# Row-wise min-max normalisation: groups of eight rows, stored whole, with VectorE kept in the written order

## Chip, cores and metric

One core of one Trainium2 chip. The metric is the device time of one execution in microseconds; a profile's span (first to last instruction) is about 1.8 us shorter. All runs quoted were in the fast state. A ratio is the mean time of one kernel's fast runs over that of the other's in the same rounds, so it is not quite the ratio of the medians quoted beside it.

## The reference

```python
def reference(x):                      # x: 32 x 512 x 1024, float32
    x_min = x.min(axis=-1, keepdims=True)
    x_max = x.max(axis=-1, keepdims=True)
    return ((x - x_min) / (x_max - x_min + 1e-8)).astype(np.float32)
```

That is 16,384 rows of 1024: 67.11 MB read once from HBM (the chip's main memory), 67.11 MB written once.

## The kernel before

Each tile has 4 rows on each of 128 partitions. GpSimd (POOL) issues the load, which casts to bf16 on the way. VectorE (DVE) halves the rows twice with a maximum and a minimum, then reduces. POOL adds and multiplies the per-row statistics, ScalarE (ACT) normalises row by row, SyncE (SP) issues two stores a tile. The order of VectorE's instructions is the scheduler's. The last 512 rows go in four small tiles.

```python
ROWS_PER_PART = 4; TT_LEVELS = 2; TAIL_TILES = 4
IN_BUFS = 7; OUT_BUFS = 4; STORE_SPLIT = 2
# ... pools cut ...
    def process(xview, oview, t, r, pool, store_rows):
        xt = pool.tile([P, r, d], bf16, name=f"xt_r{r}")
        nc.gpsimd.dma_start(out=xt, in_=xview[t])
        # ... two levels of tensor_tensor max / min, then two tensor_reduce (cut) ...
        nc.gpsimd.tensor_tensor(out=rng, in0=mx, in1=neg_mn, op=OP.add)
        nc.vector.reciprocal(out=inv, in_=rng)
        nc.gpsimd.tensor_tensor(out=nbias, in0=neg_mn, in1=inv, op=OP.mult)
        ot = out_pool.tile([P, r, d], fp32, name=f"ot_r{r}")
        for rr in range(r):
            nc.scalar.activation(out=ot[:, rr, :], in_=xt[:, rr, :], func=ACT.Identity,
                                 bias=nbias[:, rr : rr + 1], scale=inv[:, rr : rr + 1])
            if (rr + 1) % store_rows == 0:
                lo = rr + 1 - store_rows
                nc.sync.dma_start(out=oview[t, :, lo * d : (rr + 1) * d],
                                  in_=ot[:, lo : rr + 1, :])
    # ... views cut ...
    for t in range(T_main):
        process(xv, ov, t, R, in_pool, STORE_SPLIT)
    for t in range(TAIL_TILES):
        process(xvt, ovt, t, 1, tail_pool, 1)
```

Of the kernel before, what the change touches and what calls it, by code (L numbers as in the profile page):

```python
# [1 line left out]

# [4 lines left out]

ROWS_PER_PART = 4
TT_LEVELS = 2  # L10
TAIL_TILES = 4
IN_BUFS = 7
OUT_BUFS = 4
STORE_SPLIT = 2


@with_exitstack
def kernel(
    ctx: ExitStack,
    tc: tile.TileContext,  # L20
    x: bass.AP,
    out: bass.AP,
):
    nc = tc.nc
    fp32 = mybir.dt.float32
    bf16 = mybir.dt.bfloat16
    AX = mybir.AxisListType.X
    OP = mybir.AluOpType
    ACT = mybir.ActivationFunctionType

    P = nc.NUM_PARTITIONS
    R = ROWS_PER_PART

    x_flat = x.flatten_outer_dims()
    out_flat = out.flatten_outer_dims()
    n, d = x_flat.shape

    in_pool = ctx.enter_context(tc.tile_pool(name="in_pool", bufs=IN_BUFS))
    out_pool = ctx.enter_context(tc.tile_pool(name="out_pool", bufs=OUT_BUFS))
    tmp_pool = ctx.enter_context(tc.tile_pool(name="tmp_pool", bufs=2))  # L40
    stat_pool = ctx.enter_context(tc.tile_pool(name="stat_pool", bufs=10))
    tail_pool = ctx.enter_context(tc.tile_pool(name="tail_pool", bufs=TAIL_TILES + 1))

    def process(xview, oview, t, r, pool, store_rows):
        xt = pool.tile([P, r, d], bf16, name=f"xt_r{r}")
        nc.gpsimd.dma_start(out=xt, in_=xview[t])  # L46

        width = d
        cur_max = xt
        cur_min = xt  # L50
        for lvl in range(TT_LEVELS):
            half = width // 2
            nxt_max = tmp_pool.tile([P, r, half], bf16, name=f"ttmax{lvl}_r{r}")
            nc.vector.tensor_tensor(  # L54
                out=nxt_max,
                in0=cur_max[:, :, 0:half],
                in1=cur_max[:, :, half:width],
                op=OP.max,
            )
            nxt_min = tmp_pool.tile([P, r, half], bf16, name=f"ttmin{lvl}_r{r}")  # L60
            nc.vector.tensor_tensor(  # L61
                out=nxt_min,
                in0=cur_min[:, :, 0:half],
                in1=cur_min[:, :, half:width],
                op=OP.min,
            )
            cur_max, cur_min = nxt_max, nxt_min
            width = half

        mx = stat_pool.tile([P, r], fp32, name=f"mx_r{r}")  # L70
        nc.vector.tensor_reduce(out=mx, in_=cur_max, axis=AX, op=OP.max)  # L71
        neg_mn = stat_pool.tile([P, r], fp32, name=f"negmn_r{r}")
        nc.vector.tensor_reduce(  # L73
            out=neg_mn, in_=cur_min, axis=AX, op=OP.min, negate=True
        )

        rng = stat_pool.tile([P, r], fp32, name=f"rng_r{r}")
        nc.gpsimd.tensor_tensor(out=rng, in0=mx, in1=neg_mn, op=OP.add)  # L78
        inv = stat_pool.tile([P, r], fp32, name=f"inv_r{r}")
        nc.vector.reciprocal(out=inv, in_=rng)  # L80
        nbias = stat_pool.tile([P, r], fp32, name=f"nbias_r{r}")
        nc.gpsimd.tensor_tensor(out=nbias, in0=neg_mn, in1=inv, op=OP.mult)  # L82

        ot = out_pool.tile([P, r, d], fp32, name=f"ot_r{r}")
        for rr in range(r):
            nc.scalar.activation(  # L86
                out=ot[:, rr, :],
                in_=xt[:, rr, :],
                func=ACT.Identity,
                bias=nbias[:, rr : rr + 1],  # L90
                scale=inv[:, rr : rr + 1],
            )
            if (rr + 1) % store_rows == 0:
                lo = rr + 1 - store_rows
                nc.sync.dma_start(
                    out=oview[t, :, lo * d : (rr + 1) * d],
                    in_=ot[:, lo : rr + 1, :],
                )

    n_tail_rows = TAIL_TILES * P  # L100
    n_main_rows = n - n_tail_rows
    assert n_main_rows % (P * R) == 0
    T_main = n_main_rows // (P * R)

    xv = x_flat[0:n_main_rows].rearrange("(t p r) d -> t p (r d)", p=P, r=R)
    ov = out_flat[0:n_main_rows].rearrange("(t p r) d -> t p (r d)", p=P, r=R)
    for t in range(T_main):
        process(xv, ov, t, R, in_pool, STORE_SPLIT)

    xvt = x_flat[n_main_rows:n].rearrange("(t p r) d -> t p (r d)", p=P, r=1)  # L110
    ovt = out_flat[n_main_rows:n].rearrange("(t p r) d -> t p (r d)", p=P, r=1)
    for t in range(TAIL_TILES):
        process(xvt, ovt, t, 1, tail_pool, 1)


# [1 line left out]
_INS = ['x']  # L117
_OUTS = [((32, 512, 1024), 'float32')]


# [23 lines left out]
```

## Time and profile before

| | value | how to read it |
|---|---|---|
| time | 327.14 us (327.11 to 327.32) | median of 4 runs |
| span | 325.3 us | of the profiled execution |
| busiest engine | VectorE, 58% | no engine is the bound |
| 16 DMA engines | full but for the start, 20 to 31 us and the end | the bound |

The lines themselves stand in the prediction below, with what is to be seen in each. A DMA packet here is one contiguous run that one of the 16 DMA engines moves: 16 KB read for a load (8 KB written as bf16), 8 KB for a store. Shares and DMA busy times slightly over 100% come from the records of packets, which overlap a little in time.

### The profile page before, as it was taken

The page shows a single profiled execution, that of the slowest core. Times are in us where ns is not written, and L with a number is a line of the kernel's source. Part 1 is how long each engine was busy: PE and PEld are TensorE (multiplying, and loading weights), DVE is VectorE, ACT ScalarE, POOL GpSimd, SP SyncE. Part 2 cuts the span into 40 slices and gives each one's busy share as a digit, 9 for nine tenths or more (in the row PEclk, how much of TensorE's full clock was granted, in tenths as well). Part 3 has the DMA queues.
Part 4 walks back from the last instruction along what each step waited for, and adds up shares of the span by engine and source line. Part 5 has one row for each costly group of instructions (what it writes and reads, how often), then busy time and mean ns, then how long its engine had stood idle before and what let it go on. Part 6 is the DMA issues. An engine that isn't in the chain of part 4 may idle for free.

```text
span 325.3 us, 774 instructions
## 1 busy us (share of the span) xinstructions
DVE 190.0 (58%) x245; ACT 148.9 (46%) x129; POOL 60.9 (19%) x109
## 2 busy tenths in 40 slices
DVE  0899788533588443445677685577536789970000
ACT  0108953546050505235554245553355543999800
POOL 3174411210101102021101212012221042320000
DMA  6988999999999999999999999999999999999996
GB/s 124 214 178 165 282 282 299 329 309 312 285 288 279 283 284 285 288 313 313 315 312 340 314 334 295 313 329 326 333 314 312 309 334 360 430 425 429 425 430 286
DMA packets 14549, 100.71 MB, mean 310 GB/s; under 512 B 1616, under 2 KB 1616, under 8 KB 2640
## 3 DMA queue, kind: packets, MB, share of 16 engines
q0 software_dynamic: 5040, 33.56, 50.0%
q1 hardware_dynamic: 9504, 67.11, 49.8%
q14 instruction: 5, 0.04, 0.0%
HBM read 67.11 MB, written 67.11 MB: 413 GB/s over the span
## 4 chain that ended last, share of the span: by engine, by line
DMA 73%; ACT 13%; DVE 4%; issue 2%; POOL 1%; another core or an unknown queue 1%; ACTq 1%; PEldq 0%
DMA out_dram<-ot_r 71%; ACT ot_r L86 13%; DMA xt_r<-in_x_dram 2%; DVE ttmax_r L54 1%; DVE ttmin_r L61 1%; POOL rng_r L78 1%; DVE negmn_r L73 1%; DVE mx_r L71 1%; ACTq L139 0%; POOL xt_r L46 0%; ACTq L86 0%; POOL nbias_r L82 0%; PEldq L139 0%
## 5 line engine op out<-in xcount | busy, mean ns | idle before, releaser
L86 ACT ACTIVATE ot_r<-xt_r,nbias_r,inv_r 128x1024 f32<-128x1024 bf16 x128 | 147.7, 1228 | 149.5 <-DMA out_dram<-ot_r 134.9
L54 DVE TENSOR_TENSOR ttmax_r<-xt_r 128x2048 bf16<-128x2048 bf16 (+1 forms) x35 | 39.4, 1126 | 36.7 <-DMA xt_r<-in_x_dram 36.6
L46 POOL DMA_DIRECT2D xt_r<-in_x_dram x35 | 19.8, 566 | 140.1 <-ACT ot_r L86 138.9
L80 DVE RECIPROCAL inv_r<-rng_r 128x4 f32<-128x4 f32 (+1 forms) x35 | 6.1, 175 | 64.7 <-POOL rng_r L78 63.9
L71 DVE TENSOR_REDUCE mx_r<-ttmax_r 128x4 f32<-128x1024 bf16 (+1 forms) x35 | 39.1, 1117 | 0.0
L73 DVE TENSOR_REDUCE negmn_r<-ttmin_r 128x4 f32<-128x1024 bf16 (+1 forms) x35 | 39.1, 1116 | 0.0
L61 DVE TENSOR_TENSOR ttmin_r<-xt_r 128x2048 bf16<-128x2048 bf16 (+1 forms) x35 | 39.0, 1113 | 0.0
L82 POOL TENSOR_TENSOR nbias_r<-negmn_r,inv_r 128x4 f32<-128x4 f32 (+1 forms) x35 | 23.2, 666 | 40.7 <-DVE inv_r L80 40.6
L78 POOL TENSOR_TENSOR rng_r<-mx_r,negmn_r 128x4 f32<-128x4 f32 (+1 forms) x35 | 18.2, 520 | 49.7 <-DVE negmn_r L73 49.4
L61 DVE TENSOR_TENSOR ttmin_r<-ttmin_r 128x1024 bf16<-128x1024 bf16 (+1 forms) x35 | 22.3, 636 | 0.0
L54 DVE TENSOR_TENSOR ttmax_r<-ttmax_r 128x1024 bf16<-128x1024 bf16 (+1 forms) x35 | 22.2, 634 | 0.0
L86 ACT ACT_TABLE_LOAD x1 | 1.3, 1283 | 9.4 <-DMA xt_r<-in_x_dram 9.4
L128 POOL MEMSET const-float32-0.0<- 128x1 f32 x1 | 0.1, 98 | 0.2 <-issue 0.2
L128 POOL MEMSET const-bfloat16-1.0<- 128x1 bf16 x1 | 0.1, 101 | 0.0
L128 POOL MEMSET const-uint8-127<- 128x1 uint8 x1 | 0.1, 101 | 0.0
L128 POOL MEMSET const-float32-1.0<- 128x1 f32 x1 | 0.1, 98 | 0.0
## 6 DMA issues: line engine op xcount, KB each, us to landing
out_dram<-ot_r SPq DMA_DIRECT2D x62, 1024.0 KB, 33.8
xt_r<-in_x_dram POOLq DMA_DIRECT2D x31, 1024.0 KB, 12.2
out_dram<-ot_r SPq DMA_DIRECT2D x4, 512.0 KB, 12.4
xt_r<-in_x_dram POOLq DMA_DIRECT2D x4, 256.0 KB, 29.8
```

The costliest lines, as they stand in the source:

```text
L46: nc.gpsimd.dma_start(out=xt, in_=xview[t])
L54: nc.vector.tensor_tensor(out=nxt_max, in0=cur_max[:, :, 0:half], in1=cur_max[:, :, half:width], op=OP.max,)
L61: nc.vector.tensor_tensor(out=nxt_min, in0=cur_min[:, :, 0:half], in1=cur_min[:, :, half:width], op=OP.min,)
L71: nc.vector.tensor_reduce(out=mx, in_=cur_max, axis=AX, op=OP.max)
L73: nc.vector.tensor_reduce(out=neg_mn, in_=cur_min, axis=AX, op=OP.min, negate=True)
L78: nc.gpsimd.tensor_tensor(out=rng, in0=mx, in1=neg_mn, op=OP.add)
L80: nc.vector.reciprocal(out=inv, in_=rng)
L82: nc.gpsimd.tensor_tensor(out=nbias, in0=neg_mn, in1=inv, op=OP.mult)
L86: nc.scalar.activation(out=ot[:, rr, :], in_=xt[:, rr, :], func=ACT.Identity, bias=nbias[:, rr : rr + 1], scale=inv[:, rr : rr + 1],)
L128: nc = _bacc.Bacc("TRN2", target_bir_lowering=False, num_devices=1)
```

## The change

The intent is fewer and larger transfers. Two tiles become one group of 8 rows a partition, with one load and one store for the group (the first group is stored by halves, to start early); the small tail tiles go; VectorE's order is the written one. The diff, cut to its core:

```diff
-IN_BUFS = 7
+LOAD_GROUP = 2
+IN_BUFS = 3
 OUT_BUFS = 4
...
-        for t in range(T_main):
-            process(xv, ov, t, R, in_pool, STORE_SPLIT)
-        ... four small tiles ...
+    with tc.manual_schedule(engines={mybir.EngineType.DVE}):
+        RG = LOAD_GROUP * R
+        gxv = x_flat[head_rows:n].rearrange("(t p r) d -> t p r d", p=P, r=RG)
+        gov = out_flat[head_rows:n].rearrange("(t p r) d -> t p r d", p=P, r=RG)
+        for g in range(TG):
+            xtg = in_pool.tile([P, RG, d], bf16)
+            nc.gpsimd.dma_start(out=xtg, in_=gxv[g])
+            otg = out_pool.tile([P, RG, d], fp32)
+            for k in range(LOAD_GROUP):
+                rows = slice(k * R, (k + 1) * R)
+                if g == 0:  # the first group is stored by halves, to start early
+                    odst, part = gov[g, :, rows, :], otg[:, rows, :]
+                elif k == LOAD_GROUP - 1:
+                    odst, part = gov[g], otg
+                else:
+                    odst, part = None, None
+                minmax_normalize_store(xtg[:, rows, :], odst, otg[:, rows, :], part)
```

The arithmetic of a half group is that of a tile before.

More of the change, by code (lines that the diff above doesn't have):

```diff
@@ L9 @@
 ROWS_PER_PART = 4
+LOAD_GROUP = 2
 TT_LEVELS = 2
-TAIL_TILES = 4
-IN_BUFS = 7
+FP32_HEAD_TILES = 0
+IN_BUFS = 3
 OUT_BUFS = 4
-STORE_SPLIT = 2
+HEAD_BUFS = 2
 @with_exitstack
@@ L26 @@
     bf16 = mybir.dt.bfloat16
-    AX = mybir.AxisListType.X
+    AX = mybir.AxisListType
     OP = mybir.AluOpType
@@ L36 @@
     n, d = x_flat.shape
+    rows_per_tile = P * R
+    assert n % rows_per_tile == 0
+    T = n // rows_per_tile
+    xv = x_flat.rearrange("(t p r) d -> t p r d", p=P, r=R)
+    ov = out_flat.rearrange("(t p r) d -> t p r d", p=P, r=R)
     in_pool = ctx.enter_context(tc.tile_pool(name="in_pool", bufs=IN_BUFS))
+    head_pool = ctx.enter_context(tc.tile_pool(name="head_pool", bufs=HEAD_BUFS))
     out_pool = ctx.enter_context(tc.tile_pool(name="out_pool", bufs=OUT_BUFS))
@@ L41 @@
     stat_pool = ctx.enter_context(tc.tile_pool(name="stat_pool", bufs=10))
-    tail_pool = ctx.enter_context(tc.tile_pool(name="tail_pool", bufs=TAIL_TILES + 1))
-    def process(xview, oview, t, r, pool, store_rows):
-        xt = pool.tile([P, r, d], bf16, name=f"xt_r{r}")
-        nc.gpsimd.dma_start(out=xt, in_=xview[t])
-        width = d
-        cur_max = xt
-        cur_min = xt
-        for lvl in range(TT_LEVELS):
-            half = width // 2
-            nxt_max = tmp_pool.tile([P, r, half], bf16, name=f"ttmax{lvl}_r{r}")
-            nc.vector.tensor_tensor(
-                out=nxt_max,
-                in0=cur_max[:, :, 0:half],
-                in1=cur_max[:, :, half:width],
-                op=OP.max,
-            )
-            nxt_min = tmp_pool.tile([P, r, half], bf16, name=f"ttmin{lvl}_r{r}")
-            nc.vector.tensor_tensor(
-                out=nxt_min,
-                in0=cur_min[:, :, 0:half],
-                in1=cur_min[:, :, half:width],
-                op=OP.min,
-            )
-            cur_max, cur_min = nxt_max, nxt_min
-            width = half
-        mx = stat_pool.tile([P, r], fp32, name=f"mx_r{r}")
-        nc.vector.tensor_reduce(out=mx, in_=cur_max, axis=AX, op=OP.max)
-        neg_mn = stat_pool.tile([P, r], fp32, name=f"negmn_r{r}")
@@ new lines, in minmax_normalize_store @@
+    def minmax_normalize_store(xt, odst, ot, last):
+        is_bf16 = xt.dtype == bf16
+        if is_bf16:
+            width = d
+            cur_max = xt
+            cur_min = xt
+            for lvl in range(TT_LEVELS):
+                half = width // 2
+                nxt_max = tmp_pool.tile([P, R, half], bf16, name=f"ttmax{lvl}")
+                nc.vector.tensor_tensor(
+                    out=nxt_max,
+                    in0=cur_max[:, :, 0:half],
+                    in1=cur_max[:, :, half:width],
+                    op=OP.max,
+                )
+                nxt_min = tmp_pool.tile([P, R, half], bf16, name=f"ttmin{lvl}")
+                nc.vector.tensor_tensor(
+                    out=nxt_min,
+                    in0=cur_min[:, :, 0:half],
+                    in1=cur_min[:, :, half:width],
+                    op=OP.min,
+                )
+                cur_max, cur_min = nxt_max, nxt_min
+                width = half
+        else:
+            cur_max = xt
+            cur_min = xt
+        mx = stat_pool.tile([P, R], fp32)
+        nc.vector.tensor_reduce(out=mx, in_=cur_max, axis=AX.X, op=OP.max)
+        neg_mn = stat_pool.tile([P, R], fp32)
@@ L73, in process @@
         nc.vector.tensor_reduce(
-            out=neg_mn, in_=cur_min, axis=AX, op=OP.min, negate=True
+            out=neg_mn, in_=cur_min, axis=AX.X, op=OP.min, negate=True
         )
-        rng = stat_pool.tile([P, r], fp32, name=f"rng_r{r}")
+        rng = stat_pool.tile([P, R], fp32)
         nc.gpsimd.tensor_tensor(out=rng, in0=mx, in1=neg_mn, op=OP.add)
-        inv = stat_pool.tile([P, r], fp32, name=f"inv_r{r}")
+        inv = stat_pool.tile([P, R], fp32)
         nc.vector.reciprocal(out=inv, in_=rng)
-        nbias = stat_pool.tile([P, r], fp32, name=f"nbias_r{r}")
+        nbias = stat_pool.tile([P, R], fp32)
@@ L82, in process @@
         nc.gpsimd.tensor_tensor(out=nbias, in0=neg_mn, in1=inv, op=OP.mult)
-        ot = out_pool.tile([P, r, d], fp32, name=f"ot_r{r}")
-        for rr in range(r):
+        for rr in range(R):
             nc.scalar.activation(
@@ L92, in process @@
             )
-            if (rr + 1) % store_rows == 0:
-                lo = rr + 1 - store_rows
-                nc.sync.dma_start(
-                    out=oview[t, :, lo * d : (rr + 1) * d],
-                    in_=ot[:, lo : rr + 1, :],
-                )
-    n_tail_rows = TAIL_TILES * P
-    n_main_rows = n - n_tail_rows
-    assert n_main_rows % (P * R) == 0
-    T_main = n_main_rows // (P * R)
-    xv = x_flat[0:n_main_rows].rearrange("(t p r) d -> t p (r d)", p=P, r=R)
-    ov = out_flat[0:n_main_rows].rearrange("(t p r) d -> t p (r d)", p=P, r=R)
-    for t in range(T_main):
-        process(xv, ov, t, R, in_pool, STORE_SPLIT)
-    xvt = x_flat[n_main_rows:n].rearrange("(t p r) d -> t p (r d)", p=P, r=1)
-    ovt = out_flat[n_main_rows:n].rearrange("(t p r) d -> t p (r d)", p=P, r=1)
-    for t in range(TAIL_TILES):
-        process(xvt, ovt, t, 1, tail_pool, 1)
+        if odst is not None:
+            nc.sync.dma_start(out=odst, in_=last)
+    with tc.manual_schedule(engines={mybir.EngineType.DVE}):
+        H = FP32_HEAD_TILES
+        RG = LOAD_GROUP * R
+        head_rows = H * rows_per_tile
+        assert (n - head_rows) % (P * RG) == 0
+        TG = (n - head_rows) // (P * RG)
+        gxv = x_flat[head_rows:n].rearrange("(t p r) d -> t p r d", p=P, r=RG)
[10 more added lines that the diff above has]
+                    odst, part = gov[g], otg
+                else:
+                    odst, part = None, None
+                minmax_normalize_store(xtg[:, rows, :], odst, otg[:, rows, :], part)
 _INS = ['x']
```

## The prediction

> **What bounds the kernel now.** I read the page first: its busy table, the slices, the queues and the chain.
>
> ```profile
> DVE 190.0 (58%) x245; ACT 148.9 (46%) x129; POOL 60.9 (19%) x109
> ...
> DMA  6988999999999999999999999999999999999996
> GB/s 124 214 178 165 282 282 299 329 309 312 285 288 279 283 284 285 288 313 313 315 312 340 314 334 295 313 329 326 333 314 312 309 334 360 430 425 429 425 430 286
> ...
> q0 software_dynamic: 5040, 33.56, 50.0%
> q1 hardware_dynamic: 9504, 67.11, 49.8%
> ...
> HBM read 67.11 MB, written 67.11 MB: 413 GB/s over the span
> ...
> DMA 73%; ACT 13%; DVE 4%; issue 2%; POOL 1%; another core or an unknown queue 1%; ACTq 1%; PEldq 0%
> ```
>
> No engine is busy more than 58% of the span, while the 16 DMA engines are at 9 tenths in all but the first four slices and the last. The kernel is a stream: each of 67.11 MB is read and written once. The GB/s row counts what arrives, so a load counts its bf16 half; a pure load stage at 215 is 430 GB/s read. The change can win in two ways only: a higher rate while the DMA is busy, or less time in which it is not. So I asked for the DMA view of three stages: loads alone (7 to 18 us), both (80 to 140), stores alone (276 to 318), and for a table of stretches.
>
> ```profile
> DMA packets 321, 2.37 MB, mean 215 GB/s; under 512 B 32, under 2 KB 32, under 8 KB 32
> ...
> q0 software_dynamic: 321, 2.37, 103.0%
> ...
> q0 software_dynamic: 1163, 8.48, 67.5%
> q1 hardware_dynamic: 1168, 8.52, 35.0%
> ...
> DMA packets 2477, 17.90 MB, mean 426 GB/s; under 512 B 280, under 2 KB 280, under 8 KB 303
> ```
>
> ```profile
> 20.00:31.00 11.00, 10.91 (x15) 5.79 (x6) 7.31 (x8) 1.00 0.76 145
> ...
> 319.00:322.00 3.00, 0.00 (x0) 0.00 (x0) 0.00 (x0) 1.00 1.03 421
> ```
>
> In HBM bytes the rates are: loads alone 2 x 2.37 MB / 11 us = 430.9 GB/s; both, (2 x 8.48 + 8.52) / 60 = 424.7; stores alone 17.90 / 42 = 426.2; the last small stores (4 KB a packet) 421. In the mixed stage the two queues finish equally many packets (1163, 1168), so they take turns by packet; a load packet (16 KB read) costs 67.5%, a store packet (8 KB) 35.0%. Hence loads run ahead, and the end is 50 us of stores alone.
>
> Two holes in the DMA's time are visible. The start: in the chain of waits the first 2 MB load has landed at 9.33 us, and 2.10 MB at 430.9 take 4.87, so 4.5 us are lost. Then 20 to 31 us: 2 x 145 = 290 GB/s instead of 431, so 11 x (1 - 290/431) = 3.6 us lost. The timeline names its cause:
>
> ```profile
> 1.24 2.28 POOL L46 DMA_DIRECT2D xt_r<-in_x_dram  x4 [0.79 <-PEq L139]
> 15.26 3.44 POOL L78 TENSOR_TENSOR rng_r<-mx_r,negmn_r 128x4 f32<-128x4 f32 x1 [11.74 <-DVE negmn_r L73]
> 20.98 3.45 POOL L78 TENSOR_TENSOR rng_r<-mx_r,negmn_r 128x4 f32<-128x4 f32 x1 [2.28 <-DVE negmn_r L73]
> 24.36 0.58 POOL L46 DMA_DIRECT2D xt_r<-in_x_dram  x1
> ```
>
> POOL issues four loads (8.4 MB, used up by about 23 us), and its fifth stands behind two range additions, so it goes out at 24.36.
>
> **What the Trainium skill says.** "DMA: Bandwidth & Descriptors", section "Where 436 GB/s comes from", puts the fabric's ceiling at 435.2 GB/s; the trace's 424.7 to 430.9 lie just below it. The same page, "Why small descriptors are slow", gives a fixed overhead of about 3 cycles for each packet; the trace agrees in kind: at 426.2 GB/s an 8 KB store packet takes 8192 x 16 / 426.2 = 307.5 ns of one engine, at 421 a 4 KB one 155.7, so the part that does not grow with size is 2 x 155.7 - 307.5 = 3.9 ns. The same page, "Queues, rings and completion order", says that each engine goes round its queues packet by packet; the equal counts above agree. "SBUF — State Buffer", section "Who interferes with whom", says that a VectorE instruction with two SBUF inputs and a GpSimd instruction that reads SBUF exclude each other; the addition of 15.26 above lasts 3.44 us, against 0.19 at 32.93, and ends just after four such VectorE maxima and minima.
>
> **The change part by part.** Every 8 consecutive rows of a partition become one group: 16 loads of 4 MB read, 15 stores of 4 MB and two of 2 MB, in place of 35 loads and 66 stores. The built program has flat runs of 8192 elements, so a packet should be 32 KB on the HBM side for loads (16 KB before) and stores (8 KB before). The tail of four single-row tiles goes. VectorE keeps the written order, so each reciprocal waits for POOL before the next maxima start. Buffers: 3 x 16 KB in, 4 x 32 KB out, 24 KB temporaries, 200 KB a partition. Arithmetic and bytes stay.
>
> (a) Rate. Over the ideal time at 435.2 GB/s, a load packet now has 608.4 - 602.4 = 6.0 ns, a store packet 307.5 - 301.2 = 6.3. A mixed pair takes 24576 x 16 / 424.7 = 925.9 against 903.5, so 22.4: some 10 are the two switches. If this overhead is per packet, the new pair (65,536 B) takes 2409.4 + 22.4 = 2431.8 ns, 431.2 GB/s. Then 134.2 MB take 311.3 us. Now they take 325.3 - 4.5 - 3.6 - 1.7 (from the last packet to the end) = 315.5 us. Gain: 4.2 us, an estimate.
>
> (b) The hole at 20 us. Three loads, 12.6 MB, are issued at once and last 29.2 us, so till 4.5 + 29.2 = 33.7. The first group lands at about 14.2. Per half group: VectorE 5.8 us (9.35 to 15.17 in the chain), range and reciprocal 0.5, bias 0.2 to 3.5 (the lock), ScalarE 4.65. First half ready at 26 to 29, so its store reaches the queue at about 30; second half at 32 to 35, when load four goes out too. The queue barely runs dry: I keep 0.5 us of loss. Gain: 3.1 us.
>
> (c) The end. With equal packets the queues share the DMA half and half: a pair of groups takes 2 x 9.73 = 19.5 us. Worked forward by hand from (b): load 3 lands near 52, 4 near 71, 5 near 91 together with the end of store 2; ScalarE finishes group g about 18 to 19 us after it landed, in time for load g+3 and store g to queue behind a full group each. So when load 15 lands, stores 13 and 14 are still to come, 19.5 us; store 15 is ready 19.3 us after the landing, and about 2 us pass from its issue to its first packet. Loss: about 2 us of idle DMA (1.8 by these numbers), where before there was none.
>
> (d) Engines: VectorE needs 2 x 6.3 = 12.6 us a group and ScalarE 9.3, both under 19.5. The small tiles' removal saves nothing where it lies beside stores; fewer issues by POOL and SP are off the path.
>
> Sum: 327.1 - 4.2 - 3.1 + 1.8 = 321.6; I say 321.5.
>
> **The rivals.** First: the overhead is not per packet (the mixed stage loses by turning between reads and writes, whatever the size). For it: mixed is slower than either alone. Against: packets of 4 KB are slower than 8 KB without any mixing. It leaves out (a), so 325.7. Second: a wait takes the hole's place. Half the number of groups means coarser work: the last 4 MB store cannot start before its whole group is computed, and if stores do not lag two groups behind the loads when the last load lands, the DMA idles for up to a group, 9.7 us. For it: only three input groups, in-order VectorE, POOL's load waiting for ScalarE's whole group. Against: the hand-worked pace above. It costs up to 8 us more, 329. Third: VectorE becomes the bound because the lock stretches POOL's additions. Even with 3.5 us on each half the pair takes 19.6 us, just level with the DMA, so 322 to 325. Fourth, the full gain without end loss: 319.5, over the line of 2% (320.6).
>
> **Range and chances.** The centre is a gain of 1.7%, close to the line. (a) can be worth 0 to 5 us, (c) 0 to 8 with most weight near 2, (b) is the surest. I take 317.5 to 326.5. Faster by over 2% needs (a) nearly whole and an end loss under 2 us: 0.36. Slower by over 2% (333.7) needs the second rival and more: 0.03. The rest, 0.61.
>
> **What would show it.** Right: the queue table has about 2,300 packets for loads and 2,450 for stores; in the mixed stage both queues take about 50% and the bf16 bytes loaded are half of those stored; its HBM rate is near 431; slices 2 to 4 are full; pure stores at the end last some 30 us with a dip of about 2 us before the last store. Wrong on (a): packets of the old size, or 425 GB/s as before. Wrong on (c): a hole of 5 us or more in the last five slices, or repeated holes as ScalarE or POOL waits in turn. Wrong on (b): VectorE's first group landing after 16 us, or slices 3 and 4 low. The prediction as a whole falls if VectorE's busy share rises over 85%, or if the DMA's slices fall under 9 in the middle.

## The result

The changed kernel takes 319.33 us (319.23 to 319.63, 8 runs) against 327.14 (12 runs): ratio 0.9761, interval 0.9752 to 0.9771, so faster by 2.4%. The span is 317.6 us. First the slices and the queue table of the changed kernel:

```profile
DMA  6999999999999999999999999999999999999996
GB/s 132 227 204 225 332 266 297 317 343 310 322 326 330 345 288 340 314 330 332 322 313 324 326 330 312 349 312 318 322 311 359 297 330 312 343 361 433 433 425 272
...
q0 software_dynamic: 2304, 33.56, 49.9%
q1 hardware_dynamic: 2448, 67.11, 49.4%
...
HBM read 67.11 MB, written 67.11 MB: 423 GB/s over the span
```

The slices after the first are full (the third and fourth had 8 before). The packets fell from 14,544 in the two queues to 4,752; the predicted counts, some 2,300 and 2,450, are met. The stage of stores alone is now four slices long, not seven. Then the DMA view of 80 to 140 us, the mixed stage:

```profile
DMA packets 884, 19.42 MB, mean 324 GB/s; under 512 B 96, under 2 KB 96, under 8 KB 96
...
q1 hardware_dynamic: 446, 13.04, 50.9%
q0 software_dynamic: 437, 6.37, 49.7%
```

Again the queues finish equally many packets, but these now cost the same (50.9% and 49.7%, before 67.5% and 35.0%), so the two streams move at equal pace. With the packets that cross the edges of the stage shared out, the HBM rate is 431.6 GB/s (425.4 before, counted alike); the view alone, coarse at these packet sizes, gives (2 x 6.37 + 13.04) / 60 = 430. The timeline of POOL at the start answers to the one shown of before:

```profile
1.23 1.75 POOL L116 DMA_DIRECT2D xtg<-in_x_dram  x3 [0.80 <-PEq L152]
19.88 0.19 POOL L88 TENSOR_TENSOR rng<-mx,neg_mn 128x4 f32<-128x4 f32 x1 [16.90 <-DVE neg_mn L83]
20.36 1.09 POOL L92 TENSOR_TENSOR nbias<-neg_mn,inv 128x4 f32<-128x4 f32 x1 [0.29 <-DVE inv L90]
...
32.62 0.57 POOL L116 DMA_DIRECT2D xtg<-in_x_dram  x1 [4.97 <-ACT otg L95]
```

The first range addition takes 0.19 us (3.44 before), and the fourth load goes out at 32.62, just before the three loads are used up. Last, stretches of the table by windows (columns: from and to, length, VectorE, ScalarE and POOL busy, clock, DMA share, GB/s):

```profile
20.00:31.00 11.00, 10.58 (x14) 7.95 (x7) 2.45 (x4) 1.00 1.02 217
...
285.70:303.60 17.90, 11.88 (x14) 9.27 (x8) 1.69 (x4) 1.00 1.00 434
303.60:315.90 12.30, 0.00 (x0) 0.00 (x1) 0.00 (x0) 1.00 0.90 389
```

The hole at 20 to 31 us is filled (217 against 145). From 285.7, when the last load lands, to 303.6, when the last store is issued, the DMA runs at 434 GB/s: no hole there.

**The account.** For every kernel I counted, from the packets in the trace, the time in which DMA engines had no packet, averaged over the 16: the packets do not name their engine, so at each moment it is 16 less the packets under way, and never under 0. "Start" is before 5 us, "hole" 20 to 40 us, "end" after 270 us (it includes the 1.2 to 1.8 us from the last packet to the span's end); "rest" is the span less all of these and the idle time between (under 0.1 us but for the two-buffer kernel).

| kernel | time us | span us | start | hole | end | rest |
|---|---|---|---|---|---|---|
| before | 327.14 | 325.3 | 2.95 | 2.85 | 2.42 | 317.0 |
| changed | 319.33 | 317.6 | 2.88 | 0.00 | 2.44 | 312.2 |
| 8 KB runs | 329.65 | 327.7 | 3.04 | 0.02 | 5.32 | 319.3 |
| 16 KB runs | 323.97 | 322.2 | 3.00 | 0.01 | 4.50 | 314.6 |
| 16 KB runs, first stores 8 KB | 321.65 | 319.8 | 2.91 | 0.00 | 2.38 | 314.5 |
| groups of 4 rows | 321.51 | 319.6 | 2.81 | 0.00 | 2.08 | 314.7 |
| changed, scheduler's order | 329.36 | 327.5 | 2.94 | 6.68 | 3.90 | 313.9 |
| changed, 2 input buffers | 346.22 | 347.0 | 2.90 | 5.21 | 11.97 | 322.4 |
| before, loads ahead | 323.66 | 321.9 | 2.85 | 0.00 | 2.78 | 316.2 |
| before, written order | 323.81 | 322.0 | 2.90 | 0.01 | 2.66 | 316.4 |
| before, 16 KB stores | 340.80 | 339.2 | 2.96 | 2.75 | 17.04 | 316.4 |
| the same, written order | 324.21 | 322.4 | 2.91 | 0.00 | 4.36 | 315.0 |

The two-buffer kernel has another 4.5 us idle between 40 and 270 us; its profile is of its slowest run (348.73 us; they go from 344.56), which is why the span is over the median. From before to changed the span lost 7.7 us: 4.8 in the rest, 2.85 in the hole, nothing at the end. Not all of the 4.8 is the rate: the two kernels below that close the hole with the old packets ("loads ahead" and "written order") have a rest of 316.2 and 316.4, so 0.6 to 0.8 us of it go with the hole, and 4.0 to 4.2 us are left for the packets. Which part of the change gives each is what the experiments ask.

### The profile page after: what moved, and what is told of

The parts are those of the page before. It is cut to its first block, busy times and chain, and to the rows that moved or that the text cites. A ratio compares the mean times of both kernels' runs of the same rounds, so it can differ in the third digit from the quotient of the medians.

```text
span 317.6 us, 596 instructions
## 1 busy us (share of the span) xinstructions
DVE 189.8 (60%) x224; ACT 149.6 (47%) x129; POOL 38.9 (12%) x84
## 3 DMA queue, kind: packets, MB, share of 16 engines
q0 software_dynamic: 2304, 33.56, 49.9%
q1 hardware_dynamic: 2448, 67.11, 49.4%
## 4 chain that ended last, share of the span: by engine, by line
DMA 62%; DVE 18%; ACT 8%; issue 5%; POOL 2%; ACTq 0%; POOLq 0%; PEldq 0%
DMA xtg<-in_x_dram 62%; ACT otg L95 8%; DVE ttmax L61 6%; DVE ttmin L68 6%; DVE neg_mn L83 4%; DVE mx L81 1%; POOL nbias L92 1%; POOL rng L88 1%; ACTq L152 0%; DVE inv L90 0%; POOL xtg L116 0%; POOLq L152 0%; POOLq L88 0%; POOLq L116 0%; PEldq L152 0%
## 5 line engine op out<-in xcount | busy, mean ns | idle before, releaser
L95 ACT ACTIVATE otg<-xtg,nbias,inv 128x1024 f32<-128x1024 bf16 x128 | 148.3, 1229 | 140.0 <-POOL nbias L92 140.0
L61 DVE TENSOR_TENSOR ttmax<-xtg 128x2048 bf16<-128x2048 bf16 x32 | 38.7, 1208 | 94.2 <-DMA xtg<-in_x_dram 94.2
L68 DVE TENSOR_TENSOR ttmin<-xtg 128x2048 bf16<-128x2048 bf16 x32 | 39.0, 1218 | 0.0
L81 DVE TENSOR_REDUCE mx<-ttmax 128x4 f32<-128x1024 bf16 x32 | 38.7, 1210 | 0.0
L83 DVE TENSOR_REDUCE neg_mn<-ttmin 128x4 f32<-128x1024 bf16 x32 | 38.6, 1207 | 0.0
L88 POOL TENSOR_TENSOR rng<-mx,neg_mn 128x4 f32<-128x4 f32 x32 | 6.3, 197 | 185.1 <-DVE neg_mn L83 185.0
L92 POOL TENSOR_TENSOR nbias<-neg_mn,inv 128x4 f32<-128x4 f32 x32 | 23.3, 729 | 9.3 <-DVE inv L90 9.3
L68 DVE TENSOR_TENSOR ttmin<-ttmin 128x1024 bf16<-128x1024 bf16 x32 | 21.9, 683 | 0.0
L61 DVE TENSOR_TENSOR ttmax<-ttmax 128x1024 bf16<-128x1024 bf16 x32 | 21.9, 683 | 0.0
L116 POOL DMA_DIRECT2D xtg<-in_x_dram x16 | 9.1, 571 | 65.4 <-ACT otg L95 64.6
```

Source lines behind the costliest of these rows:

```text
L61: nc.vector.tensor_tensor(out=nxt_max, in0=cur_max[:, :, 0:half], in1=cur_max[:, :, half:width], op=OP.max,)
L68: nc.vector.tensor_tensor(out=nxt_min, in0=cur_min[:, :, 0:half], in1=cur_min[:, :, half:width], op=OP.min,)
L81: nc.vector.tensor_reduce(out=mx, in_=cur_max, axis=AX.X, op=OP.max)
L83: nc.vector.tensor_reduce(out=neg_mn, in_=cur_min, axis=AX.X, op=OP.min, negate=True)
L116: nc.gpsimd.dma_start(out=xtg, in_=gxv[g])
```

## The experiments

**1 and 2: packet size alone.** The changed kernel with the same groups, order, buffers and DMAs, but with a group's rows taken from four (or two) runs of HBM instead of one.

```diff
-gxv = x_flat[head_rows:n].rearrange("(t p r) d -> t p r d", p=P, r=RG)
+gxv = x_flat[head_rows:n].rearrange("(t k p r) d -> t p k r d", p=P, k=4, r=RG // 4)   # k=2 in the second
 (gov and the SBUF side of the DMAs likewise)
```

> The changed kernel with the same groups, order, buffers and number of DMAs, but each group's rows laid out in four runs of 8 KB, so that packets are 8 KB on both sides. Theory A (a packet costs some 10 ns of its engine beyond its bytes, so the rate follows the packet's size): a pair of packets takes 602.4 + 21 = 623 ns, 420.5 GB/s in the mixed stage, 134.2 MB take 319.2 us instead of 311.0, so about 327.5 us, as slow as the kernel before. Rival B (the gain is in the grouping itself: 4 MB DMAs, fewer issues, loads and stores at equal pace): 319.3 us, unchanged.

> The same with two runs of 16 KB. Theory A: a pair of packets takes 1204.7 + 21 ns, 427.7 GB/s, 313.8 us for the bytes, so about 322.1 us, a third of the way to the kernel with 8 KB runs. Rival B: 319.3 us.

Measured: 329.65 us (ratio to before 1.0069) and 323.97 (0.9897). The DMA views of 80 to 140 us, first with 8 KB runs, then with 16 KB:

```profile
q0 software_dynamic: 1591, 6.32, 51.8%
q1 hardware_dynamic: 1590, 12.63, 51.8%
```

```profile
q0 software_dynamic: 832, 6.42, 51.0%
q1 hardware_dynamic: 831, 12.83, 50.9%
```

The rates are (2 x 6.32 + 12.63) / 60 = 421.2 and 427.8 GB/s, against 420.5 and 427.7 expected; with the packets at the edges shared out, 421.1 and 428.0, and 431.6 with 32 KB. So at constant grouping the rate follows the packet's size: theory A. (329.65 us is no fair test of the grouping against the kernel before, whose loads have 16 KB packets; but experiments 4, 7 and 8 below, with 16 KB in both queues and other groupings, have 427.4 to 428.0 too.)

The cost of a packet beyond its bytes comes out alike at both steps: at 421.1, 428.0 and 431.6 GB/s a packet takes 311.3, 612.5 and 1214.8 ns of an engine, so 2 x 311.3 - 612.5 = 10.1 ns and 2 x 612.5 - 1214.8 = 10.2. In the stages of one queue the same sums give 3 to 5 ns (loads alone, 7 to 22 us: 429.7, 432.1, 433.5 GB/s; stores alone near the end: 428.3, 431.6, 433.3); so about half of the 10 ns or more comes only when the two queues alternate.

The "rest" of 319.3 us for 8 KB agrees with the 319.2 worked out; that of 16 KB is 314.6 against 313.8. Both kernels came out about 2 us over the expected time, and the account shows where: at the end (2.9 and 2.1 us more idle time than in the changed kernel), which experiment 9 takes up for the second.

**3: the hole, by loads ahead.** In the kernel before, six loads are written ahead of any arithmetic.

```diff
+AHEAD = 6
-        process(xv, ov, t, R, in_pool, STORE_SPLIT)
+        if t == 0:
+            ahead = [load(xv, i, R, in_pool) for i in range(AHEAD)]
+        elif t + AHEAD - 1 < T_main:
+            ahead.append(load(xv, t + AHEAD - 1, R, in_pool))
+        process(ahead.pop(0), ov, t, R, STORE_SPLIT)
 (load() is split off from process(); the tail is cut here)
```

> The kernel before, with its first six loads written ahead of any arithmetic (12.6 MB issued at once, as the changed kernel does); packets as before. Theory: the hole from 20 to 31 us closes, about 3 us, so 324.0 us. Rival: the hole only moves to a later place (the queue runs dry when the sixth load is done), 326 to 327 us.

Measured: 323.66 us (0.9893). The stretch that was at 0.76 and 145 GB/s before:

```profile
20.00:31.00 11.00, 11.00 (x12) 0.00 (x0) 0.00 (x0) 1.00 1.03 215
```

The hole is gone and does not reappear elsewhere.

**4: larger stores alone.** The kernel before with one store a tile.

```diff
-STORE_SPLIT = 2
+STORE_SPLIT = 4
```

> The kernel before with one store per tile instead of two, so store packets are 16 KB instead of 8 KB, all else as it was. Theory A: mixed rate 427.7 instead of 425 GB/s, stores alone about 430, some 2 us less, 325.0 us; the two queues share the engines half and half and the stage of stores alone at the end gets shorter. Rival B: no gain, 327 us, or a loss because a store starts two rows later.

Measured: 340.8 us (1.0411), 14 to 16 us over what either theory gave. Its DMA slices, then the end in the timelines of VectorE, of ScalarE and of POOL:

```profile
DMA  6979999999999999999999999999999999960697
```

```profile
298.63 1.23 DVE L54 TENSOR_TENSOR ttmax_r<-xt_r 128x2048 bf16<-128x2048 bf16 x1 [3.92 <-DMA xt_r<-in_x_dram]
299.78 0.17 DVE L80 RECIPROCAL inv_r<-rng_r 128x4 f32<-128x4 f32 x1
```

```profile
307.48 1.24 ACT L86 ACTIVATE ot_r<-xt_r,nbias_r,inv_r 128x1024 f32<-128x1024 bf16 x1 [21.32 <-POOL nbias_r L82]
```

```profile
290.22 1.09 POOL L82 TENSOR_TENSOR nbias_r<-negmn_r,inv_r 128x4 f32<-128x4 f32 x1 [4.99 <-DVE inv_r L80]
...
307.15 0.29 POOL L82 TENSOR_TENSOR nbias_r<-negmn_r,inv_r 128x1 f32<-128x1 f32 x1 [0.28 <-DVE inv_r L80]
```

Two orders of the scheduler are at work. On VectorE a tile's reciprocal stands behind the first maximum of the next tile, which waits for that tile's load. And on ScalarE: the bias of the next large tile (128x4) is ready at 291.31, but ScalarE starts only at 307.48, right after the bias of a small tile (128x1). In the built program its list has rows of two small tiles, whose arithmetic VectorE does last, ahead of the last three large tiles. So ScalarE is idle for 21.32 us around the last load, 5.1 of them before that large tile's bias was ready and 16.2 after, and the DMA is idle for some 15 us more at the end than before. In the kernel before the same kinds of order do no harm at the end, since its loads run ahead two to one and its last loads have landed by 272 us.

**8: the same with VectorE in the written order.** Besides the larger stores, the two loops go under the manual schedule.

```diff
+    with tc.manual_schedule(engines={mybir.EngineType.DVE}):
         for t in range(T_main): ...
```

> The kernel before with one store per tile (16 KB store packets, which alone made 340.8 us) and with VectorE kept in the written order. Theory C (the 13.7 us lost there came from reciprocals that stand behind the maxima of a later tile, which has not landed, so no stores were left in the queue when the loads ended): the end fills again, rate 428 GB/s, span about 2.9 + 313.8 + 2.4 and up to 3 for the two holes, 321 to 324 us. Rival E (equal pace of loads and stores itself leaves the end idle, whatever VectorE's order): about 338 us.

Measured: 324.21 us (0.9907), so it was not the equal pace by itself (rival E): order alone took 16.6 us off. That the reciprocals were the cause, as theory C has it, is not shown: the edit names VectorE alone, but in the built program ScalarE's list is back in the written order too, with the small tiles last. The trace of experiment 4 puts nearly all of the loss on ScalarE's list: its biases of the last three large tiles were ready at 291.31, 301.12 and 305.49, so with 4.65 us a tile in the written order ScalarE would have been through at about 310.4 us, an estimate, instead of 326.5; here it is at 309.6. Some idle time stays at the end (4.36).

**10: the order alone on the kernel before.**

> The kernel before with VectorE kept in the written order and nothing else, packets as before (16 KB loads, 8 KB stores). In the built program POOL's fifth load then stands behind one range addition, not two. Theory: the hole at 20 to 31 us closes (2.85 us), the rate stays at 425, the end stays full because loads run ahead two to one: 324.3 us. Rival: POOL's additions, which now each wait for a reciprocal in order, open holes elsewhere: 327 us or more.

The edit is that of experiment 8 with STORE_SPLIT left at 2. Measured: 323.81 us (0.9895). POOL's timeline at the start of this kernel:

```profile
15.27 0.19 POOL L78 TENSOR_TENSOR rng_r<-mx_r,negmn_r 128x4 f32<-128x4 f32 x1 [11.75 <-DVE negmn_r L73]
15.41 0.58 POOL L46 DMA_DIRECT2D xt_r<-in_x_dram  x1
```

Since VectorE now waits for the range addition, no maxima hold that addition up (0.19 us); the fifth load stands behind one addition and not two, and goes out at 15.41 instead of 24.36. The hole closes and the rate in the mixed stage stays (425.6 GB/s). So 3.5 of the change's 7.8 us are to be had by this one line. From here to the changed kernel the rest falls by 4.2 us.

**6: the changed kernel without it.**

```diff
-    with tc.manual_schedule(engines={mybir.EngineType.DVE}):
+    if True:
```

> The changed kernel with VectorE's order left to the scheduler, nothing else. In the built program nearly every reciprocal then stands behind the first maximum (and sometimes minimum) of the next half group, so the second half of a group can be normalised only when the next group has landed. Theory C (the stores' lag behind the loads at the end is what keeps the DMA busy there, and VectorE's order sets it): the middle of the run stays full, but the end or the start shows idle DMA of 2 to 6 us, 321 to 325 us. Rival D (VectorE is 60% busy and not the bound, so its order does not matter): 319.4 us.

Measured: 329.36 us (1.0065), slower than the kernel before and further than theory C said. The larger part, 6.7 us, is a hole at the start; in POOL's timeline of this kernel:

```profile
19.68 3.44 POOL L88 TENSOR_TENSOR rng<-mx,neg_mn 128x4 f32<-128x4 f32 x1 [16.70 <-DVE neg_mn L83]
25.40 3.45 POOL L88 TENSOR_TENSOR rng<-mx,neg_mn 128x4 f32<-128x4 f32 x1 [2.28 <-DVE neg_mn L83]
...
32.34 2.48 POOL L92 TENSOR_TENSOR nbias<-neg_mn,inv 128x4 f32<-128x4 f32 x3
...
44.12 0.57 POOL L116 DMA_DIRECT2D xtg<-in_x_dram  x1
```

The first reciprocals come at 32.1 us, behind the maxima and minima of three half groups and the first maximum of a fourth, so ScalarE frees the first input buffer late and the fourth load goes out at 44.12 instead of 32.62. In this kernel three loads at once do not close the hole without the order. (The six loads of experiment 3 are as many bytes, but there a seventh buffer let one more load go out at 18.73.)

**5: two input buffers.**

```diff
-IN_BUFS = 3
+IN_BUFS = 2
```

> The changed kernel with two input buffers instead of three. Only 8.4 MB of loads can be issued at once, they last until about 23 us, and the third load waits for ScalarE's first group, issued at 32.6 us: a hole of some 7 us at the start. After that a buffer's round (19.5 us to land in competition with a store, 18.3 to be used, 1.5 to issue, over two buffers) takes 19.7 us, just the DMA's own pace. Theory: 326 us, the loss at the start. Rival: the round is too slow in the middle as well, holes in every group, over 332 us.

Measured: 346.22 us (1.0585), as the rival had it (over 332).

```profile
DMA  7957999899998999998999899989999899999547
```

The start has its hole, but there are small ones all along, and at the end no stores are left to hide the last group. My round of 19.7 us left no slack. Besides, the packets themselves took longer: both queues' shares make (46.5% + 47.3%) x 347.0 = 325.5 us against (49.9% + 49.4%) x 317.6 = 315.4; 142 load packets and 159 store packets took over 1300 ns (62 and none in the changed kernel; the median is 1226 in both). That these are packets after a queue has run dry is likely, but not shown.

**7: small groups.**

```diff
-LOAD_GROUP = 2; IN_BUFS = 3; OUT_BUFS = 4
+LOAD_GROUP = 1; IN_BUFS = 6; OUT_BUFS = 8      # every store is of a whole group
```

> The changed kernel with groups of 4 rows instead of 8 (2 MB loads and stores, 16 KB packets on both sides, 6 input and 8 output buffers, the same bytes of buffers). Theory A by packet size: the mixed rate is the 428.0 GB/s that the kernel with two 16 KB runs showed, the bytes take 313.6 us; with the small groups the last store is only 2 MB and its arithmetic half as long, so no idle time at the end beyond the 2.4 us of the kernel before: span 2.9 + 313.6 + 2.4 = 318.9, time 320.7 us. Rival: the coarse groups cost nothing and 16 KB runs cost what they did in the kernel with two runs, 324.0 us.

Measured: 321.51 us (0.9823), 0.8 over the estimate and well under the rival's 324. At equal packet size (rest 314.7, with two runs 314.6) small groups are the better by their end: 2.08 against 4.50. The changed kernel still wins by its 32 KB packets.

**9: why the 16 KB kernel has idle time at its end and the changed kernel has none.** The windows from the landing of the last load to the last store's issue and landing, with two 16 KB runs:

```profile
291.60:309.60 18.00, 11.88 (x14) 9.27 (x8) 1.68 (x4) 1.00 0.89 381
309.60:320.50 10.90, 0.00 (x0) 0.00 (x0) 0.00 (x0) 1.00 0.91 385
```

The 18.0 us of arithmetic are those of the changed kernel (17.9), but the DMA is only 0.89 busy beside them: when the last load lands, too few stores are left; they last 17.0 us, till 308.6. The changed kernel's first two stores have 16 KB packets (half a group each) beside 32 KB loads, so at the start the loads get two thirds of the engines (67.4% against 34.0% from 43 to 56 us); here both are 16 KB (52.0% and 50.1%). Cutting the first group's stores into 8 KB packets restores that inequality:

```diff
-            nc.sync.dma_start(out=odst, in_=last)
+            if first:  # two stores of 8 KB runs
+                for j in range(2):
+                    rr = slice(2 * j, 2 * j + 2)
+                    nc.sync.dma_start(out=odst[:, :, rr, :], in_=last[:, :, rr, :])
+            else: ...
```

> The kernel with two 16 KB runs a group (323.97 us, with 2 us more idle DMA at its end than the changed kernel has), but with the first group's two stores cut into four whose packets are 8 KB, so that at the start a load packet (16 KB) meets a store packet of half its size, as in the changed kernel (32 KB against 16 KB). Theory F (the queues take turns by packet, so this first unequal stage puts the stores some 4 us further behind the loads, the lag stays through the equal stage, and at the end it is the reserve that hides the last group's arithmetic): the stores left when the last load lands last over 18 us, the idle time at the end falls from 4.5 to about 2.5 us, 322.0 us. Rival: the end is unchanged, 324 us.

Measured: 321.65 us (0.9828). The last load lands at 286.1, 5.5 us earlier, with stores left till 308.6, so for 22.5 us. The idle time at the end falls from 4.50 to 2.38 us, and the window that holds ScalarE's work on the last group is full:

```profile
290.00:310.00 20.00, 8.32 (x11) 9.27 (x8) 1.68 (x4) 1.00 1.01 431
```

Four small stores in the first 60 us moved the end: theory F. No version tried beats the changed kernel. Its rate has little left to win: at the 435.2 GB/s that the Trainium skill gives as the fabric's ceiling ("DMA: Bandwidth & Descriptors", "Where 436 GB/s comes from") its bytes would take 308.4 us, an estimate from that page's figure, and its rest is 312.2.

## Why the prediction was right

319.33 us lies in the range (317.5 to 326.5), 2.2 us under the centre; the verdict, faster by over 2%, was given 0.36, so the most likely class (within 2%) was not the one that came. Of the rivals the fourth came true, the full gain without a loss at the end: 319.5 us.

- **(a) Rate: right.** 4.2 us foretold; the rest fell by 4.8 from the kernel before and by 4.2 from that of experiment 10. 431.2 GB/s foretold for the mixed stage, 431.6 found. Experiments 1 and 2 show the per-packet part at constant grouping, and so the first rival falls. The busy time that (a) began from was small: 315.5 us against a rest of 317.0, above all since 4.5 us were taken off for the start, where the account finds 2.95 without packets. The changed kernel's was small as well (311.3 against 312.2), so the difference hardly suffered. One reading of the slices is off too: the second has 9, so only the first, third and fourth and the last are low.
- **(b) The hole: the size right, the credit incomplete.** 3.1 us foretold; 2.85 measured as time without packets, and closing it alone is worth 3.5 us (experiment 10) to 3.65 (experiment 3). The text gave the three loads issued at once as the reason, and took the written order for granted in its timing. Experiment 6 shows that in the changed kernel, with the three loads and without the order, the hole is 6.7 us, and experiment 10 that the order closes it with the old loads. Loads further ahead close it too (experiment 3).
- **(c) The end: the wrong term.** The prediction put 1.8 us of new idle time there, from 21.3 us (19.3 of arithmetic and 2 to the first packet) against 19.5 us of stores. Measured: the last load lands at 285.7, the last store is issued at 303.6, 17.9 us later, and its first packet starts at 305.03, 1.4 us after that: 19.3 us in all. The earlier stores last till 306.2, 20.5 us. The arithmetic was over-sized by 1.4 us, and so was the latency by 0.6 (its 2 us stood in the prediction without a measurement); and the reserve was 1.0 us larger than the two full stores worked with. The mechanism was right, a race between the last group's arithmetic and the stores left, but three errors of size, which happened to lie in one direction, put it on the wrong side of zero. That they cost only 2 us of the total is luck as much as skill: the range left 8 us for this term. The hand-worked landings were close (52, 71 and 91 us foretold for loads 3 to 5, 52.8, 71.6 and 91.0 found). The unequal first stage, which the working from equal packets left out, adds to that reserve: experiment 9 shows it with 16 KB packets; that it decides the margin of 1.2 us in the changed kernel is inferred from there, not shown.
- **The lock** (POOL's addition held up by VectorE's instructions with two inputs). The bias, given 0.2 to 3.5 us, takes 1.09 at the start: it waits for one maximum, not for four.
- **The second and third rivals** did not occur (VectorE 60% busy, the middle full), but experiments 5 and 6 show that the second was near: one buffer fewer or another order of VectorE brings it, at 27 and 10 us.

## What to carry to other kernels

When the DMA engines are full all along, look at the contiguous run that one packet moves, not only at the size of the DMA: with all but the first group's DMAs at 4 MB, runs of 8, 16 and 32 KB gave 421.1, 428.0 and 431.6 GB/s. Queues that take turns by packet share the engines in proportion to packet size, so changing one stream's runs shifts which stream gets ahead, and stores left over when the last load lands are the reserve that hides the last tile's arithmetic. An engine that is 60% busy can still cost 10 us by its order (experiment 6), if an instruction that frees a buffer or feeds a store stands behind work for a later tile. Read the order of every engine: here ScalarE's and POOL's lists changed too when VectorE's was fixed.

## What the Trainium skill lacked or had wrong

- "DMA: Bandwidth & Descriptors", the rules for authors: they ask for 128 partitions and at least 1 MiB a DMA for maximum bandwidth. No page has what a longer run of a packet is worth above 8 KB. With 4 MB read or written by all but the first group's DMAs in three kernels, the contiguous run still moved the mixed rate from 421.1 (8 KB) over 428.0 (16 KB) to 431.6 GB/s (32 KB).
- The same page, "Queues, rings and completion order", says that an engine switches queues by packet, but not what follows for the shares: 67.5% and 35.0% of the engines for 16 KB loads against 8 KB stores, 49.7% and 50.9% at equal size. Nor has it a cost of alternating: some 10 ns a packet with both queues at work, 3 to 5 ns with one alone.
- "SBUF — State Buffer", "SBUF: two separate sides": the loser waits for the whole instruction of the other. The runs show waits for one VectorE instruction (1.09 us) and for four in a row (3.44 us); no run here tells why.
- No page that I read has the cost of a queue that runs dry: with two input buffers the packets' own time rose from 315.4 to 325.5 us (the cause is likely, not shown).
